# Score blocks of a gated linear recurrence: seven per head, or one and three pairs from key and query copies

## The chip, the cores and the metric

The kernel runs on one core of a Trainium2 chip. Its engines are TensorE (PE: matmuls and transposes, results in PSUM), VectorE (DVE), ScalarE (ACT), GpSimd (POOL) and SyncE (SP, which here only issues DMAs). The metric is device time in microseconds (us), the median of the runs shown. A difference of about 0.3% is what a measurement of this kernel can tell from no change.

## The reference, cut to what matters

One inference step of a two-layer trunk on 640 tokens (512 latent, 128 context). Layer 0 is attention. Layer 1 is a gated linear recurrence with 8 heads, run once in each direction, with 128 key and 128 value features a head. The change lies in layer 1:

```
qh = jax.nn.silu(heads(q, REC_DK)); vh = heads(i_in, REC_DV)
forget = lb_h + (1.0 - lb_h) * jax.nn.sigmoid(z)      # for each direction
inp    = (1.0 - lb_h) * jax.nn.sigmoid(-z)            # the key
...
def step(S, xs):                       # over chunks of tokens; b is the sum of log forget
    decay  = where(mask, exp(minimum(b_t - b_s, 0)), 0)
    scores = einsum('bhtk,bhsk,bhtsk->bhts', q_i, k_i, decay)
    o_i = einsum('bhts,bhsv->bhtv', scores, v_i) + einsum('bhtk,bhkv->bhtv', q_i * exp(b_i), S)
    S   = exp(b_last)[..., None] * S + einsum('bhsk,bhsv->bhkv', k_i * exp(b_last - b_i), v_i)
...
o = _rms_norm(o_fw + flip(o_bw)); gated = o * silu(g); return gated @ w_out
```

## The kernel before, in words

Features lie on partitions. For each head `proj_gen` emits the projections: value and gate by token tiles (`vg_mms`, evacuated by `evac_vg`), then query and the two forget gates. In heads 1 to 6 the two forget gates come from seven half-size products of prepared token sums (`seven_products`, with the temporaries `c`, `u2`, `u4`); the token sums are made once, in head 0, by `token_forms`. Projection matmuls use rounded and residual parts of the operands (`rw`, `wspare`; `h1hi`, `h1lo`, `thi`, `tlo`).

The recurrence of a head is `gla_gen`. The tile `A` holds four blocks of 640 tokens: forward keys at KF, backward queries at QB, forward queries at QF, backward keys at KB. `T` and `Tb` hold products of forget gates. Scores within a 128-token tile are built by doubling. At level `lev`, of width w = 1, 2, ..., 64, neighbouring groups of w tokens are multiplied with each other (keys of one group by queries of the other, forward or backward), then keys and queries are scaled by the decay across the group, so that the next level can use groups twice as wide. A level issues:

- on PE, 20 matmuls with 32-column tiles at levels 0 to 5 and 10 with 64-column tiles at level 6, in fp32, which the profile records twice each (x40, x20), L1667 and L1673; level 0 also has the diagonal, 40 matmuls, L1680;
- on DVE, the scaling of the keys (L1683), the next decay products (L1687, shrinking from 640 to 10 columns), the scaling of the queries (L1688), and the masked merge of the scores into `near` (L1657);
- on ACT, the copy of the keys that the next level's matmuls read as stationary operand (`kcopy`, L1645, up to level 4) and, at levels 5 and 6, copies of scores into `At` (L1701).

After the levels come transposes of the keys (`kp`, L1710), chunk states (`sp`, L1716, and the sums into `S`), the output (`op`, L1733 to L1736), its norm, and a transpose (`oT`, L1753).

The recurrence of a head runs beside the projections of the next. Each `yield` of `proj_gen` gives a portion of time (1.28 or 1.6) to `Lane`, which resumes `gla_gen` when its own `yield` (D_GLA, D_LEV, ...) has fallen due. Queues are in the order that the framework makes of this: program order, with instructions that are not ready passed by others. `tc.issue_after(ins)` places later instructions of the same engine behind `ins`; a tile of a pool with one buffer for its tag waits until the tile before it in that buffer has been read for the last time. In the tail, after the last projection, each `yield` of head 7's recurrence alternates with one portion of the output projection (`tail_steps`, L1207 to L1209):

```
    lane.finish(1)
    steps = tail_steps()
    for _ in lane.gens[0][0]:
        next(steps, None)
    drain(steps)
```

`load_resid` (L1857) loads layer 0's output for the final normalization through POOL's queue.

Of the kernel before, what the change touches and what calls it, by code (L numbers as in the profile page):

```python
# [11 lines left out]
F32 = mybir.dt.float32  # L12
# [37 lines left out]
RES_AT = 6  # L50
SEVEN = range(1, RH - 1)
FORMS_AT = 3
D_GLA = 6.0
D_LEV = 2.6
D_KT = 2.0
D_ST = 3.0
D_OUT = 7.5
# [91 lines left out]
def hybrid_step(ctx: ExitStack, tc: tile.TileContext, a: dict, o: dict):  # L149
# [3 lines left out]
    def pool(name, bufs, **kw):  # L153
        return tc.tile_pool(name=name, bufs=bufs, **kw)
# [8 lines left out]
    def bank2(name, tag="b2"):  # L163
        return pools["b2"].tile([P, 2, 512], F32, tag=tag if split_banks else "b2", name=name)
# [131 lines left out]
        assert got == src, (got, src)  # L296
        return raw

    rowp = ctx.enter_context(pool("rowp", 2))

    def ada_mms(ps, sup, i):

# [128 lines left out]
    UNITS = ((0, 2), (2, 2), (4, 1))  # L431
    gate = [None, None]
    left = ctx.enter_context(ExitStack())
    right = ctx.enter_context(ExitStack())

    def lpool(name, bufs):
        return left.enter_context(pool(name, bufs))
# [884 lines left out]
    def wide(ps):  # L1322
        return ps[:].rearrange("p a b -> p (a b)")

    last_gate = []
    outs_done = []

    def held():
        st = ExitStack()
# [4 lines left out]
    def proj_gen(h, H, first):  # L1334
# [47 lines left out]
        def evac_vg(i):  # L1382
            n = 2 if i < 2 else 1
            if i == 0:
                lane.finish(2)
                assert len(lane.gens) < 2 or lane.gens[0][2], h
                H["vg"] = g2.tile([P, TT, 2, P], F32, tag="vg", name="vg")
            ps = loc.pop(("vg", i))[:, :n, :]
            low = g1.tile([P, NT], F32, tag="s", name="low")[:, :2 * CW].rearrange("p (a b) -> p a b", a=2)
            nc.scalar.copy(low[:, :n, :], ps[:, :, CW:])  # L1390
            dst = H["vg"][:, 2 * i:2 * i + n].rearrange("p t e d -> p t (e d)")
            nc.vector.tensor_tensor(dst, ps[:, :, :CW], low[:, :n, :], ALU.add)

        def mms(i, j):
            ps, hi, lo = loc[i]
# [52 lines left out]
        def seven_products():  # L1448
            fw, bw = bank2("rps", "pj"), bank2("rps", "pj")
            loc[1], loc[2] = [fw], [bw]  # L1450
            (b0, b3), (b1, b2) = ([t[:, n, :320] for n in range(2)] for t in (bw, fw))

            def block(i, j):
                return [t[:, 4 * i:4 * i + 4, slice(*HALVES[j])] for t in (h1hi, h1lo)]

            def add(out, x, y, op=ALU.add):
                nc.vector.tensor_tensor(out, x, y, op)

            t1, t2, t3, t4 = tokens
            c = g1.tile([P, NT], F32, tag="s", name="c")  # L1460
            c1, u4 = c[:, :320], c[:, 320:]
            u2 = sx.tile([P, 320], F32, tag="u2", name="u2")
            product(b1, "a11", block(0, 0))
            nc.scalar.copy(c1, b1)
            yield 1.6
            product(b2, "s2", t2)
            add(u2, c1, b2)
            yield 1.6
            product(b1, "a12", block(1, 0))
            add(b1, b1, c1)  # L1470
            yield 1.6
# [12 lines left out]
            add(b0, b0, u2, ALU.subtract)  # L1484
            evac(2)
# [109 lines left out]
    def token_forms():  # L1595
        f11, f12, f22, f21 = sums
        for f, i, j in ((f11, 0, 0), (f12, 0, 1), (f22, 1, 1), (f21, 1, 0)):
            hi, lo = (t[:, 4 * i:4 * i + 4, slice(*HALVES[j])].bitcast(F32) for t in (h1hi, h1lo))
            nc.vector.tensor_tensor(f, hi, lo, ALU.add)
            yield  # L1600
        for dst, x, y in ((f11, f12, f11), (f12, f22, f12), (f22, f11, f22)):
            nc.vector.tensor_tensor(dst, x, y, ALU.subtract)
            yield
        nc.vector.tensor_tensor(f21, f21, f22, ALU.add)
        yield
        for (hi, lo), f in zip(tokens, (f11, f22, f12, f21)):
# [27 lines left out]
    def gla_gen(h, H):  # L1634
# [6 lines left out]

        def kcopy(w):
            nb = NT // (2 * w)
            kc = g1.tile([P, NT], F32, tag="kc", name="kc")
            nc.scalar.copy(view(kc, 0, [[2 * w, nb], [w, 2], [1, w]]), view(A, KF, [[2 * w, nb], [KB - KF + w, 2], [1, w]]))  # L1645
            return kc

        yield D_GLA
        kc = kcopy(1)
        near = g1.tile([P, 32 * TT], F32, tag="near", name="near")  # L1650
        At = g1.tile([P, NT], F32, tag="At", name="At")

# [3 lines left out]
        def merge(i, pt):  # L1656
            nc.vector.copy_predicated(blocks(near[:], 32), view(masks, i * 32, [[0, TT], [1, 32]]), blocks(pt[:, :32 * TT], 32))  # L1657

        w = 1
        for lev in range(7):  # L1660
            nb = NT // (2 * w)
            pt = wide(bank2("lv"))
            for c in range(TT):
                if lev < 5:
                    for b in range(4):
                        t0 = c * P + 32 * b
                        nc.tensor.matmul(pt[32 * b:32 * b + 32, 32 * c:32 * c + 32], kc[:, t0:t0 + 32],  # L1667
                                         view(A, QB + t0, [[2 * w, 16 // w], [QF - QB + w, 2], [1, w]]), start=True, stop=True)
                else:
                    for b in range(P // w):  # L1670
                        ko, qo = (KB, QB) if b % 2 else (KF, QF)
                        s0, t0 = c * P + w * b, c * P + w * (b ^ 1)
                        nc.tensor.matmul(pt[w * b:w * b + w, w * c:w * c + w], A[:, ko + s0:ko + s0 + w], A[:, qo + t0:qo + t0 + w],  # L1673
                                         start=True, stop=True)
            if lev == 0:
                for c in range(TT):
                    for b in range(4):
                        t, o_ = slice(c * P + b * 32, c * P + (b + 1) * 32), 512 + 32 * c
                        for d, k0 in enumerate((KF, KB)):
                            nc.tensor.matmul(pt[32 * b:32 * b + 32, o_:o_ + 32], A[:, k0 + t.start:k0 + t.stop], H["q"][:, t],  # L1680
                                             start=(d == 0), stop=(d == 1))
            kv = view(A, KF, [[KB - KF + w, 2], [2 * w, nb], [1, w]])
            nc.vector.tensor_tensor(kv, kv, view(cur, 1, [[2 * nb - 1, 2], [2, nb], [0, w]]), ALU.mult)  # L1683
            if lev < 4:
                kc = kcopy(2 * w)
            qv = view(A, QB, [[QF - QB + w, 2], [2 * w, nb], [1, w]])
            nc.vector.tensor_tensor(view(nxt, 0, [[1, 2 * nb]]), view(cur, 0, [[2, 2 * nb]]), view(cur, 1, [[2, 2 * nb]]), ALU.mult)  # L1687
            last = nc.vector.tensor_tensor(qv, qv, view(cur, 2 * nb + 1, [[-2 * nb - 1, 2], [2, nb], [0, w]]), ALU.mult)  # L1688
            if lev == 0:
                nc.scalar.copy(near, pt[:, :32 * TT])  # L1690
                merge(0, pt[:, 512:])
            elif lev < 5:
                merge(lev, pt)
            if lev == 4:
                for b in range(4):
                    r = slice(32 * b, 32 * b + 32)
                    nc.gpsimd.tensor_copy(blocks(At[r, :], P)[:, :, r], blocks(near[r, :], 32))  # L1697
            elif lev > 4:
                for b in range(P // w):
                    r, o_ = slice(w * b, w * b + w), slice(w * (b ^ 1), w * (b ^ 1) + w)  # L1700
                    nc.scalar.copy(blocks(At[r, :], P)[:, :, o_], blocks(pt[r, :w * TT], w))  # L1701
            cur, nxt = nxt, cur
            w *= 2
            if lev == 6:
                residual.compute(last.ins)
            yield D_LEV
        kp = bank2("kp")
        srcs = [KF + c * P for c in (0, 1, 2, 4)] + [KB + c * P for c in (1, 2, 3, 4)]
        for i, c in enumerate(srcs):
# [8 lines left out]
        for i in range(3):  # L1718
# [2 lines left out]
            c = 3 - i  # L1721
            nc.vector.scalar_tensor_tensor(S[:, 1, c - 1, :], S[:, 1, c, :], cur[:, TT + c:TT + c + 1],
                                           spv[:, (3 + c) * P:(4 + c) * P], ALU.mult, ALU.add)
        ns = g1.tile([P, 2, P], F32, tag="kc", name="ns")
        for d in range(2):
            nc.scalar.copy(ns[:, d, :], spv[:, (3 + 4 * d) * P:(4 + 4 * d) * P])
            nc.scalar.dma_start(o["new_s"][d, h], ns[:, d, :])
# [160 lines left out]

    gate[1] = g2.tile([P, 2, D], F32, tag="A", name="gate1")
    gate_load(1, nc.gpsimd)  # L1890
    xp = lpool("xp", 1)
    load_resid(0, xp.tile([P, D], F32, name="x1"))
    load_resid(1, g2.tile([P, 2 * NT], F32, tag="T", name="x1")[:, :D])
    for tt in range(2):
        out_k(tt, 0)
    lane.finish(1)
    steps = tail_steps()
    for _ in lane.gens[0][0]:
        next(steps, None)
# [131 lines left out]
```

## Time and profile before

| | before |
|---|---|
| median of 3 runs | 831.84 us (829.66 to 832.03) |
| profiled execution, its own time | 831.37 us |
| its span, first to last instruction | 829.6 us |
| PE busy | 797.0 us, 96% |
| PE weight loads (PEld) busy | 701.8 us, 85% |
| DVE busy | 598.9 us, 72% |
| ACT busy | 428.7 us, 52% |
| POOL busy | 211.1 us, 25% |
| mean granted clock of PE | 0.996 of full |

Busy time is the sum of an engine's instructions over the whole span. Durations of matmuls overlap, so the distance between their starts says what one costs. Head 0's projection begins near 384 us, heads follow each other every 46 us or so, and the last recurrence runs beside the output projection from about 745 to 792 us.

### The profile page before, as it was taken

The numbers are of one execution on the slowest core, as the hardware profiler recorded it, in microseconds if no ns is written. First come the engines' busy times: TensorE is split into PE (matmuls) and PEld (weight loads), VectorE is DVE, ScalarE is ACT, GpSimd is POOL, SyncE is SP. The second block draws the span as 40 slices with busy tenths as digits, with TensorE's granted clock in tenths as the row PEclk, the third lists the DMA queues.
The fourth block names the chain that finished last, engine by engine and source line by source line (L and its number), as shares of the span: only waits on it lengthen the run. The fifth ranks groups of instructions, "written<-read, shape, count | busy, mean of one in ns | idle before, by whom it ended". The sixth has DMA issues, their size and how long they took to land.

```text
span 829.6 us, 19242 instructions
## 1 busy us (share of the span) xinstructions
PE 797.0 (96%) x7953; PEld 701.8 (85%) x7953; DVE 598.9 (72%) x1083; ACT 428.7 (52%) x862; POOL 211.1 (25%) x261
## 2 busy tenths in 40 slices
PE   7999999999999889999999999999999999999994
PEld 5779999888888666888899989898989989897774
DVE  4567767675677876776997686877768786868476
ACT  2252554575666775232554646547374646646242
POOL 0124001354344942101502112122312202131121
PEclk9999999999999999999999999999999999999998
DMA  9944344233140152523322342324142334325041
GB/s 327 395 145 156 102 153 145 86 128 129 51 129 26 54 176 84 196 77 100 114 78 65 96 107 77 126 67 121 46 134 66 108 95 144 100 97 170 28 157 76
DMA packets 36630, 98.12 MB, mean 118 GB/s; under 512 B 5296, under 2 KB 12480, under 8 KB 36544
## 3 DMA queue, kind: packets, MB, share of 16 engines
q1 hardware_dynamic: 25872, 78.95, 28.5%
q0 software_dynamic: 4768, 14.18, 6.0%
q10 hardware_dynamic: 5904, 3.78, 1.5%
q8 instruction: 62, 1.02, 0.5%
q14 instruction: 24, 0.20, 0.1%
HBM read 86.06 MB, written 10.83 MB: 117 GB/s over the span
## 4 chain that ended last, share of the span: by engine, by line
PE 69%; ACT 10%; DVE 10%; issue 4%; DMA 3%; POOL 2%; ACTq 1%; SPq 0%; DVEq 0%; POOLq 0%
PE pot L944 4%; PE rps L1399 4%; PE pt L1030 4%; PE rps L1400 3%; PE rps L1398 3%; PE outp L1207 3%; PE outp L1209 3%; PE outp L1208 3%; PE rps L1444 3%; PE rps L1446 3%; PE rps L1445 3%; PE lv L1667 2%; PE vgps L1376 2%; PE sc L917 2%; PE sc L918 2%
## 5 line engine op out<-in xcount | busy, mean ns | idle before, releaser
L1023 POOL TENSOR_SCALAR p<-p,rc 128x640 f32<-128x640 f32 x64 | 56.9, 894 | 114.9 <-DVE rc L1022 97.7
L1697 POOL COPY At<-near 32x160 f32<-32x160 f32 x32 | 21.2, 663 | 172.4 <-DVE T L1687 90.6
L1017 ACT ACTIVATE p<-sc,nm 128x640 f32<-128x640 f32 x64 | 51.2, 802 | 24.9 <-DVE nm L1012 15.6
L1012 DVE TENSOR_REDUCE nm<-sc 128x1 f32<-128x640 f32 x64 | 51.7, 817 | 12.8 <-PE sc L918 12.5
L1399 PE MATMUL rps<-h1lo,rw 128*128 128x320 f32 x176 | 55.3, 314 | 0.0
L1400 PE MATMUL rps<-h1hi,rw 128*128 128x320 f32 x176 | 55.0, 312 | 0.0
L1398 PE MATMUL rps<-h1hi,rw 128*128 128x320 f32 x176 | 54.9, 312 | 0.0
L1645 ACT COPY kc<-A 128x640 f32<-128x640 f32 x40 | 32.1, 802 | 43.8 <-DVE A L1683 42.5
L1030 PE MATMUL pt<-small,p 128*128 128x128 f32 x320 | 48.9, 277 | 2.8 <-DVE pts L922 1.2
L1376 PE MATMUL vgps<-rw,h1hi 128*128 128x512 f32 x180 | 48.9, 396 | 0.0
L1030 PEld LDWEIGHTS pt<-small,p 128*128 128x128 f32 x320 | 36.5, 140 | 11.5 <-issue 5.7
L917 PE MATMUL sc<-kk,X 128*128 128x320 f32 x128 | 42.4, 340 | 1.7 <-ACT p L1017 1.6
L922 ACT COPY pts<-pt 128x512 f32<-128x512 f32 x64 | 36.1, 590 | 15.1 <-PE pt L1030 15.0
L944 PE MATMUL pot<-pts,vv 128*64 128x256 f32 x320 | 38.3, 384 | 2.1 <-DVE pts L922 2.0
L374 PE MATMUL gps<-hhi,whi 128*128 128x320 f32 x128 | 40.0, 312 | 0.1
L375 PE MATMUL gps<-hlo,whi 128*128 128x320 f32 x128 | 39.6, 309 | 0.0
L376 PE MATMUL gps<-hhi,wlo 128*128 128x320 f32 x128 | 39.5, 309 | 0.0
L1376 PE MATMUL vgps<-wspare,h1hi 128*128 128x512 f32 x140 | 38.3, 394 | 0.6 <-issue 0.6
L1376 PEld LDWEIGHTS vgps<-rw,h1hi 128*128 128x128 f32 x180 | 32.8, 188 | 7.0 <-ACT s L1509 0.2
L918 PE MATMUL sc<-klo,X 128*128 128x320 f32 x128 | 38.6, 310 | 0.0
L207 POOL TENSOR_TENSOR rstdo<-rs_t,mhalf 128x5 f32<-128x5 f32 x8 | 9.7, 1213 | 103.2 <-DVE rs_t L206 103.2
L383 PE MATMUL qmm<-whi,hhi 128*128 128x256 f32 x120 | 35.0, 292 | 0.1
(342 smaller groups left out, 2599.0 us busy)
## 6 DMA issues: line engine op xcount, KB each, us to landing
raw<-in_rec_w_in SPq DMA_DIRECT2D x40, 512.0 KB, 3.8
raw<-in_ada_m SPq DMA_DIRECT2D x16, 512.0 KB, 8.0
raw<-in_attn_w_in SPq DMA_DIRECT2D x16, 512.0 KB, 5.0
raw<-in_ada_s SPq DMA_DIRECT2D x16, 512.0 KB, 3.8
adaraw<-in_ada_c SPq DMA_DIRECT2D x11, 512.0 KB, 5.3
raw<-in_attn_w_out SPq DMA_DIRECT2D x8, 512.0 KB, 3.9
raw<-in_rec_w_out SPq DMA_DIRECT2D x8, 512.0 KB, 3.7
raw<-in_ada_c SPq DMA_DIRECT2D x5, 512.0 KB, 4.1
```

Of the source, the lines that this page charges most:

```text
L374: nc.tensor.matmul(ps[:, :320], w.hi(k)[:, c], hhi[:, k, t], start=(k == 0), stop=False)
L917: nc.tensor.matmul(out, X[:, h, t0:t0 + P], kk[:, c, k0:k1], start=True, stop=False)
L918: nc.tensor.matmul(out, X[:, h, t0:t0 + P], klo[:, c, k0:k1], start=False, stop=True)
L944: nc.tensor.matmul(pot[j * HD:(j + 1) * HD, :CW], vv[:, slot, c * HD:(c + 1) * HD], moving[j], start=first, stop=last)
L1012: nc.vector.tensor_reduce(nm[:, 0:1], sc[:, :, :320], AX.XY, ALU.max, negate=True)
L1017: return nc.scalar.activation(halves(p[:]), sc[:, :, :320], AF.Exp, bias=nm[:, 0:1], accum_out=su[:, 0:1])
L1023: nc.gpsimd.tensor_scalar(p, p, rs[:, 0:1], 1.0, ALU.mult, ALU.mult)
L1030: nc.tensor.transpose(pt[:, i * 256 + q * P:i * 256 + (q + 1) * P], ps[q][:, (k0 + i) * P:(k0 + i + 1) * P], ident)
L1376: nc.tensor.matmul(out, h1hi[:, k, t], wvg[i][:, k % 4].rearrange("p e n -> p (e n)"), start=(k == 0), stop=(k == KT - 1))
L1398: nc.tensor.matmul(ps[:, j, :320], hi[:, k, :], h1hi[:, k, t], start=(k == 0), stop=False)
L1399: nc.tensor.matmul(ps[:, j, :320], hi[:, k, :], h1lo[:, k, t], start=False, stop=False)
L1400: nc.tensor.matmul(ps[:, j, :320], lo[:, k, :], h1hi[:, k, t], start=False, stop=(k == KT - 1))
```

## The change

The levels are issued in four blocks: level 0 with the diagonal, then levels 1 and 2, 3 and 4, 5 and 6. `decay` scales keys and queries for one level. The first level of a pair reads a copy of the keys and a copy of the queries (`qcopy`, new), taken before the scaling of that level; the second reads a key copy and `A` as before (level 6 `A` alone). `kcopy` makes one copy more a head and has two buffers; the first is made before the first `yield`. The query copy and `u2` of `seven_products` share one buffer (tag `qc`). The yields between blocks are 2 x D_LEV; D_GLA goes from 6.0 to 5.5 and D_LEV from 2.6 to 2.7. The four sums of `token_forms` are placed behind the latest evacuation of `vg`. The tile for the first residual takes a buffer of tag `vg`, its load and the second one's are issued behind `lane.finish(1)`, and the pool `rowp` moves to the other side of the memory.

```diff
-D_GLA = 6.0
-D_LEV = 2.6
+D_GLA = 5.5
+D_LEV = 2.7
...
-    rowp = ctx.enter_context(pool("rowp", 2))
+    right = ctx.enter_context(ExitStack())
+    rowp = right.enter_context(pool("rowp", 2, side="right"))
...
-            nc.vector.tensor_tensor(dst, ps[:, :, :CW], low[:, :n, :], ALU.add)
+            vg_done[:] = [nc.vector.tensor_tensor(dst, ps[:, :, :CW], low[:, :n, :], ALU.add).ins]
...
-            u2 = sx.tile([P, 320], F32, tag="u2", name="u2")
+            u2 = g1.tile([P, NT], F32, tag="qc", name="u2")[:, :320]
...
-            nc.vector.tensor_tensor(f, hi, lo, ALU.add)
+            with tc.issue_after(vg_done[0]):
+                nc.vector.tensor_tensor(f, hi, lo, ALU.add)
...
-            kc = g1.tile([P, NT], F32, tag="kc", name="kc")
+            kc = g1.tile([P, NT], F32, tag="kc", name="kc", bufs=2)
...
+        def qcopy(w):
+            nb = NT // (2 * w)
+            qc = g1.tile([P, NT], F32, tag="qc", name="qc")
+            nc.scalar.copy(view(qc, 0, [[2 * w, nb], [w, 2], [1, w]]), view(A, QB, [[2 * w, nb], [QF - QB + w, 2], [1, w]]))
+            return qc
+
+        kc = kcopy(1)
         yield D_GLA
-        kc = kcopy(1)
...
-        w = 1
-        for lev in range(7):
-            nb = NT // (2 * w)
-            pt = wide(bank2("lv"))
+        def scores(pt, lev, kc, qc):
+            w = 1 << lev
             for c in range(TT):
                 if lev < 5:
                     for b in range(4):
                         t0 = c * P + 32 * b
...
+                        q = qc[:, t0:t0 + 32] if qc else view(A, QB + t0, [[2 * w, 16 // w], [QF - QB + w, 2], [1, w]])
+                        nc.tensor.matmul(pt[32 * b:32 * b + 32, 32 * c:32 * c + 32], kc[:, t0:t0 + 32], q, start=True, stop=True)
...
+        def decay(lev, snap):
+            nonlocal cur, nxt
+            w = 1 << lev
+            nb = NT // (2 * w)
+            kc = qc = None
             kv = view(A, KF, [[KB - KF + w, 2], [2 * w, nb], [1, w]])
             nc.vector.tensor_tensor(kv, kv, view(cur, 1, [[2 * nb - 1, 2], [2, nb], [0, w]]), ALU.mult)
-            if lev < 4:
+            if lev < 5:
                 kc = kcopy(2 * w)
...
             last = nc.vector.tensor_tensor(qv, qv, view(cur, 2 * nb + 1, [[-2 * nb - 1, 2], [2, nb], [0, w]]), ALU.mult)
...
+            if snap:
+                qc = qcopy(2 * w)
+            cur, nxt = nxt, cur
+            return kc, qc, last
...
+        pt = wide(bank2("lv"))
+        scores(pt, 0, kc, None)
+        diagonal(pt[:, 512:])
+        k1, q1, _ = decay(0, True)
+        nc.scalar.copy(near, pt[:, :32 * TT])
+        merge(0, pt[:, 512:])
+        for lev in (1, 3, 5):
+            k2, _, _ = decay(lev, False)
+            yield 2 * D_LEV
+            pt = wide(bank2("lv"))
+            scores(pt, lev, k1, q1)
+            scores(pt[:, 512:], lev + 1, k2, None)
+            k1, q1, last = decay(lev + 1, lev < 5)
+            place(lev, pt)
+            place(lev + 1, pt[:, 512:])
+        residual.compute(last.ins)
+        yield D_LEV
...
-    xp = lpool("xp", 1)
-    load_resid(0, xp.tile([P, D], F32, name="x1"))
-    load_resid(1, g2.tile([P, 2 * NT], F32, tag="T", name="x1")[:, :D])
     for tt in range(2):
         out_k(tt, 0)
     lane.finish(1)
+    load_resid(0, g2.tile([P, 2 * NT], F32, tag="vg", name="x1")[:, :D])
+    load_resid(1, g2.tile([P, 2 * NT], F32, tag="T", name="x1")[:, :D])
```

## Rows read from the trace of the kernel before

**Rows 1.** The page's first part: busy us (share of the span) xinstructions.

```profile
PE 797.0 (96%) x7953; PEld 701.8 (85%) x7953; DVE 598.9 (72%) x1083; ACT 428.7 (52%) x862; POOL 211.1 (25%) x261
```

**Rows 2.** Windows A:B: length, busy us of each engine, clock, DMA share.

```profile
515.00:560.00 45.00, 44.66 (x599) 40.95 (x598) 34.44 (x59) 25.04 (x51) 9.53 (x14) 1.00 0.30 92
745.00:791.60 46.60, 44.25 (x541) 35.67 (x539) 26.29 (x50) 21.45 (x55) 8.20 (x13) 1.00 0.32 104
```

**Rows 3.** Timeline of PE around one level block: start us, us, instruction.

```profile
532.38 0.31 PE L1398 MATMUL rps<-h1hi,rw 128*128 128x320 f32 x1
532.62 0.56 PE L1667 MATMUL lv<-A,kc 128*32 128x32 f32 x40
...
533.37 0.30 PE L1400 MATMUL rps<-h1hi,rw 128*128 128x320 f32 x1
...
534.83 0.31 PE L1398 MATMUL rps<-h1hi,rw 128*128 128x320 f32 x1
```

**Rows 4.** Timeline of PE at a first level with its diagonal.

```profile
570.09 0.63 PE L1667 MATMUL lv<-A,kc 128*32 128x32 f32 x40
570.53 1.01 PE L1680 MATMUL lv<-q,A 128*32 128x32 f32 x80
```

**Rows 5.** Waits of PE for others: us in total, times, longest us.

```profile
PE lv L1667 <- DVE A L1688: 1.3, 6, 0.5
PE lv L1673 <- DVE A L1688: 1.2, 1, 1.2
PE lv L1667 <- ACT kc L1645: 1.2, 5, 0.5
```

**Rows 6.** Timeline of the tail: level 3's block, level 4's key product and block.

```profile
766.19 0.56 PE L1667 MATMUL lv<-A,kc 128*32 128x32 f32 x40
...
769.33 0.82 DVE L1683 TENSOR_TENSOR A<-A,T 128x640 f32<-128x640 f32 x1
769.63 0.56 PE L1667 MATMUL lv<-A,kc 128*32 128x32 f32 x40
```

**Rows 7.** Timeline of PE at a block of level 6.

```profile
499.43 0.80 PE L1673 MATMUL lv<-A 128*64 128x64 f32 x20
...
500.41 0.31 PE L1445 MATMUL rps<-h1lo,rw 128*128 128x320 f32 x1
```

**Rows 8.** The key copy's line: min/median/max ns; who waited for it (us, times).

```profile
L1645 ACT COPY kc<-A x40: 717/730/1037, 426.7 to 767.7; 128x640 f32<-128x640 f32 x40
...
  DVE A L1688: 12.3, 17
```

**Rows 9.** Timeline of DVE and PE in head 0, at the token sums.

```profile
396.70 2.01 DVE L1599 TENSOR_TENSOR f<-h1hi,h1lo 128x1280 f32<-128x1280 f32 x1
...
400.30 0.68 DVE L1392 TENSOR_TENSOR vg<-vgps,low 128x512 f32<-128x512 f32 x1
...
401.03 0.41 PE L1398 MATMUL rps<-h1hi,wspare 128*128 128x320 f32 x1 [2.05 <-DVE vg L1392]
```

**Rows 10.** DVE: all additions into u, and in one head level 4's queries and additions.

```profile
L1457 DVE TENSOR_TENSOR u<-c,rps x6: 475/475/489, 453.5 to 684.5; 128x320 f32<-128x320 f32 x6
...
541.65 0.83 DVE L1688 TENSOR_TENSOR A<-A,T 128x640 f32<-128x640 f32 x1
...
545.03 0.47 DVE L1457 TENSOR_TENSOR u<-c,rps 128x320 f32<-128x320 f32 x1
...
557.16 0.49 DVE L1457 TENSOR_TENSOR rps<-rps,u 128x320 f32<-128x320 f32 x1
```

**Rows 11.** Timeline of the tail's start; the residual's loads (KB each, us to landing).

```profile
749.40 1.07 POOL L1857 DMA_DIRECT2D x<-x1a  x2
749.90 0.82 ACT L1510 ACTIVATE A<-s,omlb 128x640 f32<-128x640 f32 x1
...
752.25 1.02 ACT L1645 COPY kc<-A 128x640 f32<-128x640 f32 x1
...
x<-x1a POOLq DMA_DIRECT2D x5, 512.0 KB, 6.1
```

More of the change, by code (lines that the diff above doesn't have):

```diff
@@ L433, in hybrid_step @@
     left = ctx.enter_context(ExitStack())
-    right = ctx.enter_context(ExitStack())
     def lpool(name, bufs):
@@ L1326, in hybrid_step @@
     outs_done = []
+    vg_done = []
     def held():
@@ L1666, in gla_gen @@
                         t0 = c * P + 32 * b
-                        nc.tensor.matmul(pt[32 * b:32 * b + 32, 32 * c:32 * c + 32], kc[:, t0:t0 + 32],
-                                         view(A, QB + t0, [[2 * w, 16 // w], [QF - QB + w, 2], [1, w]]), start=True, stop=True)
+                        q = qc[:, t0:t0 + 32] if qc else view(A, QB + t0, [[2 * w, 16 // w], [QF - QB + w, 2], [1, w]])
+                        nc.tensor.matmul(pt[32 * b:32 * b + 32, 32 * c:32 * c + 32], kc[:, t0:t0 + 32], q, start=True, stop=True)
                 else:
@@ L1672, in gla_gen, with diagonal @@
                         s0, t0 = c * P + w * b, c * P + w * (b ^ 1)
[L1673 to L1681, printed above, removed]
+                        k, q = (kc, qc) if qc else (A[:, ko:ko + NT], A[:, qo:qo + NT])
+                        nc.tensor.matmul(pt[w * b:w * b + w, w * c:w * c + w], k[:, s0:s0 + w], q[:, t0:t0 + w], start=True, stop=True)
+        def diagonal(pt):
+            for c in range(TT):
+                for b in range(4):
+                    t, o_ = slice(c * P + b * 32, c * P + (b + 1) * 32), 32 * c
+                    for d, k0 in enumerate((KF, KB)):
+                        nc.tensor.matmul(pt[32 * b:32 * b + 32, o_:o_ + 32], A[:, k0 + t.start:k0 + t.stop], H["q"][:, t],
+                                         start=(d == 0), stop=(d == 1))
+        def decay(lev, snap):
[3 more added lines that the diff above has]
+            kc = qc = None
             kv = view(A, KF, [[KB - KF + w, 2], [2 * w, nb], [1, w]])
             nc.vector.tensor_tensor(kv, kv, view(cur, 1, [[2 * nb - 1, 2], [2, nb], [0, w]]), ALU.mult)
-            if lev < 4:
+            if lev < 5:
                 kc = kcopy(2 * w)
@@ L1688, in gla_gen, with place @@
             last = nc.vector.tensor_tensor(qv, qv, view(cur, 2 * nb + 1, [[-2 * nb - 1, 2], [2, nb], [0, w]]), ALU.mult)
[L1689 to L1692, printed above, removed]
+            if snap:
+                qc = qcopy(2 * w)
+            cur, nxt = nxt, cur
+            return kc, qc, last
+        def place(lev, pt):
+            w = 1 << lev
+            if lev < 5:
                 merge(lev, pt)
@@ L1701, in gla_gen @@
                     nc.scalar.copy(blocks(At[r, :], P)[:, :, o_], blocks(pt[r, :w * TT], w))
[L1702 to L1706, printed above, removed]
+        pt = wide(bank2("lv"))
[15 more added lines that the diff above has]
+        yield D_LEV
         kp = bank2("kp")
@@ L1723, in gla_gen @@
                                            spv[:, (3 + c) * P:(4 + c) * P], ALU.mult, ALU.add)
-        ns = g1.tile([P, 2, P], F32, tag="kc", name="ns")
+        ns = g1.tile([P, 2, P], F32, tag="kc", name="ns", bufs=2)
         for d in range(2):
```

## The prediction

> **What bounds the kernel now.** I read the page's busy shares first [rows 1]: TensorE (PE) is busy for 797.0 of the 829.6 us. Then the windows of the recurrence [rows 2]: in a 45 us stretch, about one head, PE stands idle for only 0.34 us, at full granted clock, while VectorE (DVE) works 34.4 and ScalarE (ACT) 25.0 us. So a head costs what its PE instructions occupy, and a wait elsewhere counts only where PE runs out of other matmuls. But busy is not all useful, and for that the starts of matmuls are read, not their durations. In the PE timeline around one level block [rows 3], ten projection matmuls start between 533.37 and 534.83, one each 0.146 us. The block starts 0.24 us after the projection matmul at 532.38, and the second one behind it comes at 533.37. That is 0.99 us; less two ordinary steps (0.29) the lone block costs 0.70. In a longer block [rows 4] the next part starts 0.44 us after 40 records of the same size. So of 0.70 us some 0.25 is getting in and out.
>
> Last I read the waits. PE's waits in front of level blocks are few [rows 5]: 1.2 us for the key copy, 1.3 and 1.2 for the scaled A. The chain from one level to the next (key product on DVE, key copy on ACT, query product on DVE, next block) is read in the tail [rows 6], where little else is on DVE and ACT: block at 766.19, next at 769.63, 3.44 us. Elsewhere projection matmuls fill that time.
>
> **The change, part by part.** The sum is made for the profiled execution, 831.37 us (1.77 more than its span; the median of the runs shown is 0.47 above it).
>
> *Seven blocks become four.* No matmul is added or dropped. In pairs 1+2 and 3+4 the second level costs 0.44 us in place of 0.70: I take 0.25 each. Level 6 uses 64-column tiles [rows 7]: 0.98 from 499.43 to 500.41, with the entry of 0.24 and less two steps 0.93 us. Whether joining 32-column to 64-column tiles saves a whole passage no row shows. Bounds: all of it, 0.25; or an inner switch as dear as the 0.09 of entry and 0.10 of exit by which the steps around a block exceed an ordinary one, so 0.06 is left. I take the middle, 0.16. That is 0.66 a head. Heads 0 to 6 lie inside PE-bound projections: 7 x 0.66 = 4.6 us (bounds 3.9 and 5.2). Head 7 lies in the tail, below.
>
> The stretched steps around a block [rows 3] show that a passage costs something, without naming why. The Trainium skill, page "TensorEngine Tiling (Array Packing)", section Tiling Modes, says that a change of tiling mode, though not of tile, drains the engine. By that rule the switch from 128x32 to 128x64 inside the last pair still drains, and this term would be 3.9; were only the passage from and to the projections dear, 5.2. No row here tells these apart.
>
> *The first key copy moves ahead of the yield,* so ACT makes it when A is written, not when the block is due. That removes PE's wait for it: five times, 1.2 us [rows 5]. The state loads on ACT's queue precede it in either version. What it now stands in front of are ACT's casts of the next head's weights; a copy is 0.73 us [rows 8], and ACT's 20 idle us in 45 [rows 2] cover it; without them the casts, and PE behind them, would be 0.73 late. I take -1.2 (0 if ACT is occupied all the same).
>
> *The due times.* Working through the lane's steps of 1.28 and 1.6, the first block still falls due at 6.4 of the head's time (5.5 and 6.0 both lie between the steps 5.12 and 6.40), the pairs at 11.52, 17.6 and 22.4, where levels 2, 4 and 6 were, and the key transposes at 25.6, as before. So levels 1, 3 and 5 go later and nothing behind them moves. The six waits for the scaled A add up to 1.3 us, the longest 0.5 [rows 5]; half of the 0.8 beside the longest I count as gone: -0.4 (bounds 0 and -0.8).
>
> *More copies.* A head gets one more key copy and three query copies, 4 x 0.73 = 2.9 us of ACT, 25 to 28 of 45; DVE's work is unchanged. DVE's query product waited 17 times, 12.3 us, for a key copy [rows 8], though the two touch different parts of A; so strided views of A wait for each other, and I expect a key product to wait for the query copy also. A pair's chain is then two level chains, 6.88, less the middle block and its hand-off (0.69), plus 0.44 for the longer block and 0.86 for the query copy with its hand-off: 7.5 us. Outside the tail that has cover: PE has projections, and the transposes' due time is the same. Behind the copies in ACT's order stand casts and evacuations; when those are late, PE waits. I charge +0.3; the bounds are 0 and the first rival.
>
> *Token sums behind vg.* In head 0 [rows 9] DVE's first sum at 396.70 holds the engine for 2 us, then comes a split, the second vg addition only at 400.30, and PE starts the query at 401.03 after a wait of 2.05. With the edge the sums come behind the third vg addition. The split may still go first, so I take -1.7 (bounds 0 and -2.05). The four sums come some 3 us later; what needs them is not the query but the seven products of the next heads, whose first addition is at 453.5 [rows 10], 50 us off. Without that room the products would be 3 us late.
>
> *The tail.* Head 7 has only out-projection matmuls beside it, one portion for each yield, and there are three yields less; what is left over is issued behind. From 745 to 791.6 PE idles 2.35 us [rows 2], 0.5 and 1.2 of it in front of level blocks [rows 5]. The chain: up to the second block one middle block goes and one query copy comes, +0.2; the next pair 7.5 for 6.9, +0.6; the last, where the key product of level 4 began before its block (769.33, 769.63) [rows 6], about +0.3; the last block is longer by 0.5. That is +1.6. The first copy comes earlier: A is finished at 750.72 and the copy ran at 752.25 [rows 11]; I take -1.1. Net +0.5, and the 0.66 of PE time is not cashed. If the products do not wait for query copies, three times 0.86 less: -2.
>
> *At nothing:* the x1 load of tile 0 goes behind head 6's last steps on POOL's queue. It was issued at 749.40 and takes 6.1 us [rows 11]; it is needed only when head 7's recurrence is over, and level 4's block is at 769.63 [rows 6]. These 20 us cover it; without them the load's 6.1 us would show. The row pool on the other side only shifts addresses.
>
> Sum: -4.6 -1.2 -0.4 +0.3 -1.7 +0.5 = -7.1, so 824.3 us.
>
> **The rivals.** *The waits come back.* A pair needs two DVE rounds and two or three copies before its block, and a late one stops PE at 24 pair blocks. For it: the copies stand in an engine that works in order, between casts. Against it: other matmuls fill the 3.44 us between blocks today, and all of PE's waits for levels are 3.7 us in 56 blocks. At 0.16 us a block (the 0.8 of five small waits) it gives back 3.8: 828.1. At 0.30 the gain is gone: 831.5.
>
> *The query copy collides with u (slower).* The query copy and the products' temporary u share one buffer, in six heads. The copy for level 5 must get in ahead of u's first write, at 545.03 in one head [rows 10]; the query product that it follows ended at 542.48, 2.5 us earlier, and my chain up to there is 0.8 longer. Once it is later by 1.7 us more, the order turns: level 5 then waits until the last addition, over at 557.65, some 14 us. The next head's projections hide part of it. If 2 to 3 us a head remain, 6 heads cost 12 to 18, and with -7.1 the time is 836 to 842. Against it: the copy comes first in the program.
>
> *More than the sum.* Three round trips between PE and DVE vanish from each head's chain. If strided copies do not hold the products, the tail loses its 2.35 us of idle and cashes its 0.66, and the +0.5 goes: 820.8.
>
> **How the numbers follow.** Forecast 0.62, with its own range 821.5 to 828.5 (bounds: pairs 3.9 to 5.2, head 0 from 0 to 2.05, first copy 0 to 1.2, tail -2 to +2); waits come back to 829 or more 0.17; collision 0.11; more 0.10. A measurement tells about 0.3%, 2.5 us, from no change. Faster: 0.62 + 0.10 = 0.72; the same 0.17; slower 0.11. The range takes in the larger gain and the returned waits up to no change: 819 to 832.
>
> **What would show it.** Four level blocks a head on PE; 1.1 to 1.2 us of cost for a joined pair of 32-column levels, in place of 1.40; no wait of PE for the first key copy; the query of head 0 starting near 399; ACT about 28 us in 45; a head's period shorter by 0.66 to 0.9. Wrong: waits of PE for kc, qc or A growing past 3.7 us, u's first addition ahead of the fourth block, or a level chain in head 7 longer by more than 2 us.

## The result: slower by 2.6 us, where 7 us less were forecast

The changed kernel takes 835.1 us (median of 22 runs, 832.4 to 839.6), the kernel before on the same chip 832.95 us. The ratio is 1.0031, with a 95% interval of 1.0017 to 1.0045: about 2.6 us slower (1.4 to 3.7). Forecast were 824.3 us.

The profiled execution of the changed kernel has a span of 836.6 us, 7.0 more than that of before. Milestones split it: 2.44 us arise before head 0's projection begins, a place that the change's matmuls do not touch (granted clock 0.97 in the first 100 us, 1.00 in the kernel before; the kernels below reach that point anywhere between 382.3 and 387.3); head 0, up to its key transposes, gains 0.48; the six head periods behind it gain 0.02; the rest, from head 6's key transposes to the end, is 5.06 longer. So one execution overstates the loss; its place, the tail, is what to read.

The windows of the changed kernel (columns as in [rows 2]; the third is about six heads):

```profile
515.00:560.00 45.00, 44.74 (x599) 41.00 (x599) 35.05 (x59) 27.41 (x55) 9.35 (x14) 1.00 0.30 91
745.00:795.00 50.00, 43.95 (x544) 35.86 (x543) 26.82 (x50) 24.29 (x59) 8.79 (x13) 0.97 0.33 106
460.00:740.00 280.00, 277.89 (x3663) 255.01 (x3662) 211.81 (x355) 177.73 (x344) 63.27 (x96) 1.00 0.34 98
```

In a head PE is as busy as before, and ACT has grown to 27.4 us, as forecast. In the tail PE idles 6.05 us of 50, where it idled 2.35 of 46.6. Next, PE's timeline where levels 3 to 6 of one head stand:

```profile
538.94 0.56 PE L1674 MATMUL lv<-qc,kc 128*32 128x32 f32 x40
...
540.65 0.56 PE L1674 MATMUL lv<-A,kc 128*32 128x32 f32 x40
...
544.35 0.33 PE L1680 MATMUL lv<-qc,kc 128*32 128x32 f32 x14
...
546.56 0.44 PE L1680 MATMUL lv<-qc,kc 128*32 128x32 f32 x26
546.93 0.80 PE L1680 MATMUL lv<-A 128*64 128x64 f32 x20
```

This is the main finding: **pairs 1+2 and 3+4 do not exist on the engine.** Levels 3 and 4 (qc and A as right operands) stand 1.7 us apart with projections between; level 5 is cut in two, and only its second part touches level 6. So it is in heads 1 to 5; in head 0 levels 5 and 6 stand apart, and only in heads 6 and 7 is this last pair whole. The program emits a pair as one block, but each instruction gets its place by when its own operands are there. The first level reads copies that are early; the second waits for the scaling. The order of the built program, before any run, is already so. One head (position on PE, with a run of like instructions counted as one; x20 are twenty instructions); the seven rows are levels 1, 2, 3, 4, two parts of 5, and 6, and other matmuls stand wherever the position jumps:

```
2386 L1674 MATMUL lv<-qc,kc 32x32 x20
2389 L1674 MATMUL lv<-A,kc 32x32 x20
2427 L1674 MATMUL lv<-qc,kc 32x32 x20
2435 L1674 MATMUL lv<-A,kc 32x32 x20
2455 L1680 MATMUL lv<-qc,kc 32x32 x7
2468 L1680 MATMUL lv<-qc,kc 32x32 x13
2469 L1680 MATMUL lv<-A 64x64 x10
```

So heads 0 to 5 have seven blocks each, as before, and as many passages in and out are paid; six heads cost the same. Why level 5 is cut no run shows: it is cut in e5 and e12 below too, where all its operands are there together. The first matmul of the key transposes of heads 0 and 6, before and after:

```profile
456.50 0.71 PE L1710 MATMUL kp<-small,A 128*128 128x128 f32 x5
734.20 0.60 PE L1710 MATMUL kp<-small,A 128*128 128x128 f32 x4
```

```profile
458.46 0.71 PE L1740 MATMUL kp<-small,A 128*128 128x128 f32 x5
736.14 0.60 PE L1740 MATMUL kp<-small,A 128*128 128x128 f32 x4
```

277.70 us became 277.68. PE's waits in the recurrence (us in total, times, longest), to be held against [rows 5]:

```profile
PE lv L1674 <- DVE A L1701: 2.5, 7, 0.7
PE lv L1674 <- ACT qc L1653: 2.1, 1, 2.1
...
PE op L1766 <- DVE S L1752: 1.3, 1, 1.3
...
PE sp L1746 <- ACT kt L1742: 1.1, 1, 1.1
...
PE kp L1740 <- DVE A L1696: 0.9, 1, 0.9
```

The waits for kc are gone; between 440 and 740, where they were 1.2 us, those for the scaled A have grown from 0.8 to 2.1. The last three, and the 2.1, are new and all in the tail. There, on PE:

```profile
762.45 0.56 PE L1674 MATMUL lv<-qc,kc 128*32 128x32 f32 x40 [2.12 <-ACT qc L1653]
...
764.29 0.63 PE L1207 MATMUL outp<-rw,ghi 128*128 128x512 f32 x1
764.72 0.63 PE L1208 MATMUL outp<-rw,ghi 128*128 128x512 f32 x1
...
776.41 0.39 PE L1209 MATMUL outp<-w,glo 128*128 128x512 f32 x1
...
777.86 0.80 PE L1680 MATMUL lv<-A 128*64 128x64 f32 x20 [0.47 <-DVE A L1701]
779.59 1.09 PE L1740 MATMUL kp<-small,A 128*128 128x128 f32 x8 [0.93 <-DVE A L1696]
781.83 2.05 PE L1746 MATMUL sp<-vg,kt 128*128 128x128 f32 x16 [1.15 <-ACT kt L1742]
...
785.61 0.49 PE L1766 MATMUL op<-S,A 128*128 128x128 f32 x2 [1.28 <-DVE S L1752]
```

Between 776.41 and 788.09 no out-projection matmul (outp) is issued: with three yields fewer, the portions that stood between kp, sp and op before now come behind them, and PE waits for each hand-over. In the kernel before, one follows the transposes of head 7 at once:

```profile
776.12 1.04 PE L1710 MATMUL kp<-small,A 128*128 128x128 f32 x8
776.91 0.48 PE L1207 MATMUL outp<-wx,ghi 128*128 128x512 f32 x1
```

These transposes (776.12, now 779.59) split the tail's 5.06 us: counted from head 6's, 1.53 arise ahead of them, in the level chain, and 3.53 behind. At 762.45 the query copy is late, since it stood on ACT behind a weight cast that itself waited for its DMA:

```profile
760.66 1.05 ACT L256 CAST w<-raw 128x1024 fp32r<-128x1024 f32 x1 [1.57 <-DMA raw<-in_rec_w_out]
761.61 0.79 ACT L1653 COPY qc<-A 128x640 f32<-128x640 f32 x1
```

### The profile page after: what moved, and what is told of

The parts are those of the page before. It is cut to its first block, busy times and chain, and to the rows that moved or that the text cites. A ratio compares the mean times of both kernels' runs of the same rounds, so it can differ in the third digit from the quotient of the medians.

```text
span 836.6 us, 19239 instructions
## 1 busy us (share of the span) xinstructions
PE 802.4 (96%) x7953; PEld 705.8 (84%) x7953; DVE 599.6 (72%) x1083; ACT 449.0 (54%) x894; POOL 208.1 (25%) x261
## 4 chain that ended last, share of the span: by engine, by line
PE 63%; DVE 16%; ACT 9%; issue 4%; DMA 3%; POOL 2%; ACTq 0%; SPq 0%; DVEq 0%; POOLq 0%
PE outp L1207 4%; PE outp L1208 4%; PE outp L1209 4%; PE pot L944 3%; PE pt L1030 3%; PE rps L1445 3%; PE acc L562 3%; PE rps L1399 3%; PE rps L1400 3%; PE rps L1447 3%; PE rps L1446 3%; PE rps L1401 2%; PE sc L917 2%; PE gps L375 2%; PE gps L377 2%
## 5 line engine op out<-in xcount | busy, mean ns | idle before, releaser
L1023 POOL TENSOR_SCALAR p<-p,rc 128x640 f32<-128x640 f32 x64 | 56.8, 894 | 117.6 <-DVE rc L1022 100.3
L1647 ACT COPY kc<-A 128x640 f32<-128x640 f32 x48 | 38.3, 798 | 38.5 <-DVE A L1696 23.5
L1377 PE MATMUL vgps<-wspare,h1hi 128*128 128x512 f32 x140 | 40.8, 401 | 0.0
```

What stands on the lines that cost most here:

```text
L1023: nc.gpsimd.tensor_scalar(p, p, rs[:, 0:1], 1.0, ALU.mult, ALU.mult)
L1377: nc.tensor.matmul(out, h1hi[:, k, t], wvg[i][:, k % 4].rearrange("p e n -> p (e n)"), start=(k == 0), stop=(k == KT - 1))
```

## The experiments

Each kernel is the one named, with the edit shown. "Six heads" runs from head 0's key transposes to head 6's, "rest" from there to the end of the span, both of the profiled run. The ratio is to runs of the kernel before taken beside each experiment, whose medians lie between 832.16 and 833.8: ratios can be compared, medians only roughly. e5, e10 and e12 compute other scores, as said there.

| kernel | median us | ratio (95%) | six heads | rest |
|---|---|---|---|---|
| before | 832.95 | 1 | 277.70 | 95.4 |
| after | 835.1 | 1.0031 (1.0017 to 1.0045) | 277.68 | 100.5 |
| e1_glue | 843.14 | 1.0131 (1.0108 to 1.0155) | 283.36 | 99.4 |
| e2_tail | 833.16 | 1.0018 (0.9997 to 1.0039) | 277.18 | 97.2 |
| e3_both | 841.01 | 1.0105 (1.0080 to 1.0131) | 283.58 | 100.3 |
| e4_edge | 831.48 | 0.9988 (0.9969 to 1.0008) | 277.52 | 95.4 |
| e5_same | 834.09 | 1.0012 (0.9997 to 1.0027) | 277.42 | 97.6 |
| e6_copies | 834.08 | 1.0006 (0.9989 to 1.0023) | 278.17 | 98.1 |
| e7_short | 836.44 | 1.0044 (1.0020 to 1.0069) | 277.34 | 101.2 |
| e8_first | 831.47 | 0.9981 (0.9965 to 0.9997) | 277.39 | 95.7 |
| e9_late | 852.79 | 1.0233 (1.0210 to 1.0256) | 284.75 | 106.5 |
| e10_same_c | 834.84 | 1.0016 (1.0002 to 1.0031) | 276.59 | 99.5 |
| e11_all | 848.61 | 1.0187 (1.0168 to 1.0206) | 284.80 | 103.0 |
| e12_same_order | 829.21 | 0.9943 (0.9923 to 0.9963) | 273.76 | 97.5 |
| e13_all2 | 836.99 | 1.0044 (1.0027 to 1.0060) | 279.87 | 98.9 |

**Pairs made real (e1_glue, after).** Every matmul of a pair's first level also waits for the second level's scaling, so that both are ready together.

```diff
-            k2, _, _ = decay(lev, False)
+            k2, _, both = decay(lev, False)
-            scores(pt, lev, k1, q1)
+            scores(pt, lev, k1, q1, both.ins)   # add_manual_dep(mm.ins, after.name, ...) on each matmul
```

> The changed kernel, with each matmul of a pair's first level also waiting for the second level's queries, so that the two levels can only be issued together. Theory (the pairs were never issued as pairs, so no passage in and out of a level block was saved): the 6 head periods between the key transposes of heads 0 and 6 shrink from 277.7 us by 0.25 for each passage saved, two a head at the least, so by 2.5 to 4 us, and the whole lands within 1.5 us of the kernel before. Rival (a passage costs nothing that PE could use, or the first level's later start brings waits): the periods stay at 277.7 within 0.5 and the whole stays 2 to 4 us above the kernel before.

Pairs 1+2 and 3+4 stand joined, 5 with nine tenths of 6; the last tenth stands alone, but for heads 6 and 7. PE waits instead:

```profile
PE lv L1671 <- DVE A L1707: 16.6, 18, 1.8
```

A head takes 47.2 us in place of 46.3. Neither expectation has the number; the second one names the cause, waits from the later start. The prediction's rival "the waits come back" is real once there are pairs, at 0.7 us a pair block (16.6 in 24) and not 0.16: the block stands where the plan puts it, before its scalings are done.

**The portions back (e2_tail, after), and both (e3_both).**

```diff
-    for _ in lane.gens[0][0]:
-        next(steps, None)
+    for n, _ in enumerate(lane.gens[0][0]):
+        for _ in range(2 if n in (2, 3, 4) else 1):
+            next(steps, None)
```

> The changed kernel, with the twelve portions of the output projection spread over the nine yields of the last head (two portions after three of them), as they stood against the levels before. Theory (in the tail PE ran out of portions before the last output block, because three yields are gone): PE's idle time in the tail falls from 6.0 to 3 us or less, and the whole from 2.6 us above the kernel before to 1 us below it, or equal. Rival (the tail is longer because the level chain with its query copies is longer): the key transposes and the output of head 7 come as late as in the changed kernel, and the whole stays 2 to 4 us above the kernel before.

> Both edits together. Theory: the two gains add, 2.5 to 4 us from the heads and 3 to 4 us from the tail, so 3 to 5 us below the kernel before (ratio 0.994 to 0.997). Rival: no faster than the kernel before by more than 1 us.

In e2 the waits in front of sp and op are gone, PE idles 2.76 us from 745 to 795 in place of 6.05, and the rest is 3.3 us shorter; what is left is mostly in front of score blocks:

```profile
PE lv L1674 <- ACT qc L1653: 1.1, 1, 1.1
PE lv L1674 <- DVE A L1701: 0.7, 1, 0.7
PE lv L1680 <- ACT qc L1653: 0.5, 1, 0.5
```

The part behind head 7's transposes is as in the kernel before (53.6 us; 53.5 before, 57.0 in the changed kernel); the part ahead of them stays 1.75 longer. In the measured ratios the gain over the changed kernel (0.0013) is smaller than either interval. With the glue as well (e3), the heads' loss stays, and the rival holds.

**One part alone (e4_edge, before + the edge on the token sums).**

```diff
+            with tc.issue_after(vg_done[0]):
                 nc.vector.tensor_tensor(f, hi, lo, ALU.add)
```

> The kernel before with the one edge that places the four token sums behind the evacuation of vg. Theory (it takes away a wait of PE in head 0 that nothing else hides): the wait of 2.05 us in front of the query falls to about 0.6, and the whole is 1 to 1.5 us shorter (ratio 0.998 to 0.999). Rival (VectorE is the bound in head 0, and the sums come back as a later wait of PE): the wait falls as well, but head 0's key transposes come as late as before, and the whole is unchanged.

The query's wait of 2.05 [rows 9] is 0.67; of the 1.38 gained there, 0.56 is given back by head 0's transposes. The ratio says 1 us, and its interval includes no change at all.

**Joined without any wait (e5_same, after).** The second level of a pair multiplies the copies of the first, so it need not wait; its scores lack a scaling and are other numbers.

```diff
-            scores(pt[:, 512:], lev + 1, k2, None)
+            scores(pt[:, 512:], lev + 1, k1, q1)
```

> The changed kernel, but the second level of each of the three pairs multiplies the first level's copies (k1 and q1), so both levels of a pair are ready at the same moment and nothing has to wait for the second level's scaling; the scores of levels 2, 4 and 6 are then other numbers. Theory (the blocks were not joined because the second level's operands came later, and joining itself is worth the 0.66 us a head of the forecast): the two blocks stand side by side on TensorE, six heads take about 277.7 - 6 x 0.66 = 273.7 us, and the time is about 835.1 - 4.6 = 830.5. Rival (a joined block saves nothing, or the scaling chain sets the pace): six heads stay at 277.5 to 277.8 and the time at 834 to 836.

PE does its work in 273.39 us instead of 277.89 (the same window of 280 us as above), 0.74 less a head, and the heads are no shorter: a new wait has taken it, once a head.

```profile
460.00:740.00 280.00, 273.39 (x3665) 254.33 (x3665) 211.20 (x357) 179.04 (x344) 66.96 (x96) 1.00 0.33 98
```

```profile
PE rps L1445 <- ACT c L1465: 6.5, 6, 1.2
```

The third product needs the bank that ACT empties into c. The theory held for PE's work and fell for the time, where the rival was right. The last pair is cut here too, in heads 0 to 5, mostly behind 54 of its 60 records.

**The copies alone (e6_copies), the missing portions alone (e7_short), the small parts alone (e8_first), all from before.** e6 and e8 also load x1 where the changed kernel does.

```diff
+            if lev in (0, 2, 4):        # e6: copies that nobody reads, u2 in their buffer
+                qcopy(2 * w)
...
+        if n not in (2, 3, 4):          # e7
             next(steps, None)
...
+        kc = kcopy(1)                   # e8, with bufs=2 and the edge of e4
         yield D_GLA
-        kc = kcopy(1)
```

> The kernel before with the three query copies of each head added (nobody reads them), u2 in the copies' buffer and x1 loaded where the changed kernel loads it; every score block as before. Theory (the copies are hidden in the heads and cost only in the tail, where ScalarE stands in the chain): six heads 277.5 to 277.8, the tail longer by 0 to 1.5 us, time 833 to 834.5 against 832.95 for the kernel before. Rival (each copy is in the way of the key copies and of TensorE): 3 x 0.7 us in each head, six heads above 280, time above 840.

> The kernel before with the output projection's portions left out after three of the tail's yields (they come after the last head instead), so that as many portions stand between the last head's steps as in the changed kernel. Theory (the tail lost its cover): the transposes, the state products and the output products of the last head wait 0.9, 1.2 and 1.3 us as in the changed kernel, time 834.5 to 836. Rival (the portions are only moved, and what the changed kernel lost lies in the query copies and the clock): 832.5 to 833.5.

> The kernel before with only the token sums behind the last gate value (as in the edge experiment) and the first key copy made before the yield, in two buffers, and x1 loaded where the changed kernel loads it; no query copies, levels one by one, due times as before. Theory (both are small gains): the edge gave a ratio of 0.9988, the first copy is worth up to 1.2 us by the forecast, time 830.5 to 831.5, ratio 0.997 to 0.9985. Rival (in the tail the first copy comes no earlier than before, as in the changed kernel, and what the sums gain is lost again by the first transposes): ratio 0.9988 to 1.000.

The copies cost nothing that the runs can tell from 0 (six heads 0.5 us, rest 2.7 in one profile, 2.5 of it ahead of head 7's transposes). The missing portions cost 3.7 us (1.7 to 5.7) by themselves, as their theory had it, with the waits of the changed kernel:

```profile
PE op L1736 <- DVE S L1722: 1.2, 1, 1.2
...
PE sp L1716 <- ACT kt L1712: 1.1, 1, 1.1
PE kp L1710 <- ACT At L1701: 1.0, 1, 1.0
```

and with the granted clock down behind that idle time (windows of 5 us, e7_short, then the changed kernel behind its wait of 2.12 us):

```profile
775.00:780.00 5.00, 2.89 (x18) 2.38 (x15) 1.56 (x2) 1.85 (x3) 0.00 (x0) 0.62 0.01 3
780.00:785.00 5.00, 3.76 (x21) 3.57 (x20) 1.64 (x6) 0.17 (x2) 0.00 (x0) 0.70 0.00 0
```

```profile
760.00:765.00 5.00, 2.88 (x49) 2.14 (x48) 3.46 (x6) 3.41 (x4) 0.00 (x0) 0.91 0.19 66
765.00:770.00 5.00, 5.00 (x56) 3.64 (x56) 4.11 (x9) 0.80 (x2) 0.00 (x0) 0.75 0.00 0
```

The edge with the early first copy is the only version of the reference's computation whose interval lies wholly below 1: 1.6 us (0.25 to 2.9) faster than the kernel before.

**Later due times (e9_late, e1 + D_GLA 4.5, D_LEV 3.4, D_ST 1.5).**

> The joined kernel of the glue experiment with other due times: the yield behind the first copy 4.5 instead of 5.5, D_LEV 3.4 instead of 2.7 and D_ST 1.5 instead of 3.0, so that a pair is planned behind 6.8 us of projection instead of 5.4. Theory (the 16.6 us of waits in the glue experiment came from pairs planned before their scalings could be done): the waits of the score blocks fall below 5 us in all and six heads from 283.4 to 277.5 or less; whether they come below 277 depends on the wait for the first product's copy that took the gain in the run with equal operands; time 833 to 836. Rival (the scalings of two levels take longer than any place in the head allows): six heads above 280, time above 839.

The score blocks' waits between 440 and 740 fell from 12.8 us (e1) to 3.6, as the theory had it, and the heads grew all the same. The cut of D_ST, part of this edit, made a new wait, of 0.8 us a head; with the 0.6 of the blocks, in place of 0.4 a head in the changed kernel, that explains most, not all, of the heads' growth of 1.2:

```profile
PE op L1772 <- DVE S L1758: 4.9, 5, 1.3
PE lv L1671 <- DVE A L1707: 3.2, 6, 0.6
```

**c in its own buffer (e10_same_c, e5 +; e11_all, e9 + this and e2).** The buffer that c shared is held by the query's sigmoid until DVE has multiplied the query.

```diff
-            c1, u4 = c[:, :320], c[:, 320:]
+            c1, u4 = g1.tile([P, D], F32, tag="kt", name="c1")[:, :320], c[:, 320:]
```

> The kernel whose second level of a pair uses the first level's copies (scores of levels 2, 4 and 6 are other numbers), and the first product's copy c1 in a buffer of its own (that of the key transposes) instead of the one that holds the query's sigmoid. Theory (the 0.7 us a head that the joined blocks save went into the product matmuls' wait for c1, whose buffer is held until VectorE has multiplied the query behind the scalings): that wait of 1.1 us a head goes, six heads take 273 to 275 us, time 830 to 832. Rival (the next thing in line holds TensorE, VectorE or ScalarE being as late with the following steps): another wait of 0.5 to 1.1 us a head, six heads 276.5 to 277.5, time 833 to 834.5.

> The joined kernel with the later due times, c1 in a buffer of its own, and the tail's portions where they stood before (two after three of the yields); the computation is the reference's. Theory (three causes, each taken away: pairs planned too early, c1 held by the query's sigmoid, portions that ran out): six heads 273.5 to 275.5, the tail from the seventh head's transposes to the end 97 us, time 829 to 832. Rival (the waits for the scalings stay, or a new one takes the gain): six heads 277 or more, time 833 or more.

The wait is 0.9 a head and not 1.1, and six heads are 0.8 us shorter than in e5: the buffer was a small part of it, and six heads lie in the rival's range. The time did not fall. ACT is what is late now; from the query copy to c it works without a pause (e10_same_c):

```profile
542.29 0.73 ACT L1653 COPY qc<-A 128x640 f32<-128x640 f32 x1 [0.94 <-DVE A L1701]
542.93 0.70 ACT L1497 ACTIVATE s<-rps 128x640 f32<-128x640 f32 x1
543.52 0.61 ACT L1410 CAST rw<-a 128x512 fp32r<-128x512 f32 x1
544.03 0.43 ACT L1465 COPY c<-rps 128x320 f32<-128x320 f32 x1
```

e11_all kept e9's D_ST, and with it the wait of op, 4.9 us; it says nothing on c1.

**The cast behind c (e12_same_order, e10 +).** The cast of a22 serves only the last product; its step now comes after the first product's.

```diff
+            with tc.issue_after(loc["c1"]):      # the copy of c1
                 split_pair(wr.tile([P, 2, 1024], F32R, tag="w", name="rw"), a22, ("a22",))
```

> The kernel whose second level of a pair uses the first level's copies (scores of levels 2, 4 and 6 are other numbers), with c1 in its own buffer and now also ScalarE's cast of a22, which only the last product needs, issued behind the copy of c1. Theory (what is left of the product matmuls' wait, 0.9 us a head, is ScalarE's queue: query copy, sigmoid and cast stand ahead of c1): the wait falls by the cast's 0.5 us to 0.3 to 0.5 a head, six heads from 276.6 to 273.5 to 274.5, time 830 to 832.5. Rival (VectorE's queue in the same stretch, with the scalings, is as late, and the next product waits for it): another wait takes the 0.5 us, six heads 276 to 277, time 833.5 to 835.

The theory held: the wait is 2.4 us in six heads, and six heads take 273.76 us. PE has no wait for c in the changed kernel, so the two edits on c by themselves had none to remove there; they were not run without the joining.

```profile
456.71 0.49 PE L1744 MATMUL kp<-small,A 128*128 128x128 f32 x3
...
535.31 0.31 PE L1401 MATMUL rps<-h1hi,rw 128*128 128x320 f32 x1
535.55 0.90 PE L1678 MATMUL lv<-qc,kc 128*32 128x32 f32 x80
536.38 0.41 PE L1399 MATMUL rps<-h1hi,rw 128*128 128x320 f32 x1
536.63 0.31 PE L1400 MATMUL rps<-h1lo,rw 128*128 128x320 f32 x1
...
730.47 0.71 PE L1744 MATMUL kp<-small,A 128*128 128x128 f32 x5
```

From 535.31 to 536.63, less two steps of 0.146, a joined pair costs 1.03 us, where two lone blocks cost 1.40. The last pair is again cut in heads 0 to 5 (34 records and 26).

**The same with true operands (e13_all2, e1 + D_GLA 3.0 and D_LEV 3.3, c1, the cast, the portions).**

> The joined kernel with the true operands (each block of a pair waits for the second level's scaling), planned later (D_GLA 3.0, D_LEV 3.3, D_ST 3.0 again, since 1.5 let the output products wait 0.8 us a head for the states), c1 in its own buffer, the cast of a22 behind c1, and the tail's portions where they stood before; the computation is the reference's. Theory (the rest of the loss in the two later-planned runs was D_ST and the product's copy): the output products wait no more, the score blocks below 4 us in all, six heads 275 to 277, time 831 to 834. Rival (two levels of scalings in a row are longer than what a head leaves between its blocks, wherever they are planned): six heads above 279, time above 837.

Between 440 and 740 the score blocks wait 2.8 us and op for S no more. Four of the six head periods are 46.2 to 46.3, as in the kernel before; the other two are 47.0 and 47.8. In one of the four (593.88 to 640.16) PE is busy for 45.73 us, where a head of the changed kernel takes 46.02 (550.99 to 597.29): 0.3 less and not 0.66, with 0.3 more idle time in its place. Pairs 1+2 and 3+4 are joined, but the last pair stands in three parts (34 records, 24 and 2), two passages more than a whole pair has. In head 7, which has few matmuls beside it, the waits are longer (this row is the whole run; head 7 has 4.4 of it, in two waits):

```profile
PE lv L1675 <- DVE A L1711: 6.5, 8, 3.4
```

Neither expectation is met in full, though six heads (279.87) and the time lie at the rival's numbers.

## Why the prediction was wrong, point by point

- **The step that failed is "Seven blocks become four", -4.6.** Its premise was wrong: that blocks emitted together are issued together. The prediction priced the group and did not ask of each instruction when it may issue, though the queues' order is told in the section on the kernel before. With its own operands each level is issued when it is ready, and the term is 0 (277.70 and 277.68). When the pairs are forced, the second level's scaling stops PE, and even without that, the third product's wait for c took the whole gain (e5): the bound next in line, ACT's and DVE's queues at the query's end, was not looked for.
- **The price of that step came out right in part by luck.** Six heads of e12 are 3.92 us shorter, 0.65 a head against 0.66, but not from the parts of the sum. A pair of 32-column levels saves 0.37 and not 0.25: behind a first level the 40 records of a second add 0.33, not the 0.44 that was read from level 0 [rows 4]. The last pair saves 0.20 where it is whole, as in head 6 of the changed kernel, against the 0.16 taken, but in five of the six heads of e12 it is cut. Whole pairs throughout would have made 0.94 a head by these prices; no run has them.

```profile
731.05 0.31 PE L1401 MATMUL rps<-h1hi,rw 128*128 128x320 f32 x1
731.29 0.56 PE L1680 MATMUL lv<-qc,kc 128*32 128x32 f32 x40
731.78 0.80 PE L1680 MATMUL lv<-A 128*64 128x64 f32 x20
...
732.77 0.31 PE L1400 MATMUL rps<-h1lo,rw 128*128 128x320 f32 x1
```

- **Rival "the waits come back".** In the heads of the changed kernel it did not happen (2.3 us in place of 2.0), since nothing was joined. In e1 it did, at 0.7 us a pair block. The sign named for it, waits for kc, qc or A past 3.7 us, was seen all the same: 5.3 in the whole run, by the tail's 2.1 and 0.5.
- **The tail, +0.5.** It was +5.1 in the profiled execution. The prediction named the three lost yields and took the leftover portions to be "issued behind" at no price; e7 puts 3.7 us on them alone, and of the 5.06 us the 3.53 behind head 7's transposes are gone in e2. That they are the cover of kp, sp and op should have been read from the tail's timeline. Ahead of the transposes it is +1.53: the longer chain was priced at 1.6, about right, and the 1.1 taken off for an earlier first copy did not come. That the chain has the forecast length is partly luck, since its term of 0.2 for a query copy stood against a wait of 2.12 behind a cast. How much of this is the copies' is not settled: 2.5 in e6's profile, under 1.9 us by the upper end of its ratio's interval.
- **First key copy, -1.2, and due times, -0.4.** PE's waits between 440 and 740 were 1.2 for kc and 0.8 for A; they are 2.3 for A and a copy. The cause of the wait was moved, not removed. In the tail the first copy came no earlier. The due times alone were not tried.
- **Token sums, -1.7.** -1.43 at the query, of which 0.95 is gone again at head 0's transposes. Edge and first copy together are 1.6 us in e8.
- **More copies, +0.3.** ACT 27.4 us in 45, heads unchanged: right. DVE's key product does wait for the query copy (3.7 us, 7 times), without stopping PE in the heads, and the wait of 14 us for u that the second rival feared did not occur.
- **Together.** e8, e7 and e6 make -0.0019 + 0.0044 + 0.0006 = +0.0031, the ratio measured. The agreement is closer than their intervals allow one to trust; e2, which puts the portions back, gains 0.0013 and not 0.0044.

## What to carry to other kernels

A group of matmuls in the program was a group on the engine here only where its last operand came no later than its first, and the last pair was cut even so; ask of each instruction when it may issue, and read the built order, before pricing the group as one. When a step is taken out of a chain that paces other work by its yields, count what each yield used to bring and where that cover stood. And a saving on the busiest engine is worth what the next queue lets through: here ScalarE had no pause at one place of each head, though it idles some 18 us of 45.

## What the runs showed of the hardware

- *The granted clock can fall behind short idle times.* Behind PE's idle of 2.12 us the clock is 0.91 and then 0.75 of full in the windows above, and portions' matmuls start every 0.43 us (764.29, 764.72) instead of 0.23: the lower level, 1.2 in place of 2.4 GHz. An estimate from these two windows, (0.09 + 0.25) x 5 us, puts 1.7 us of the tail's loss on it. In e7 the clock is 0.62 and 0.70 behind waits of 1.0, 1.1 and 1.2 us. In e2, with waits of 1.1 and 0.7 in the same stretch, it stays at 1.00; and so it does in the changed kernel behind its waits of 0.93, 1.15 and 1.28. No run shows what tells these cases apart.
- *Going from 32-column to 64-column tiles costs a good part of a passage.* Lone, level 5 and level 6 cost 0.70 and 0.93 us; joined, from 731.05 to 732.77 less two steps of 0.146, they cost 1.43. That saves 0.20, where joining two 32-column levels saves 0.37. So the change of width costs 0.17 of the 0.37, and the saving lies between the prediction's bounds of 0.06 and 0.25. The Trainium skill, page "TensorEngine Tiling (Array Packing)", section Tiling Modes, lets a change of mode drain the engine and a change of tile not. The trace agrees in direction with this 0.17.
